# A decoder kernel: nine of each layer's weight low parts are subtracted on GpSimd instead of VectorE

## The chip, the cores and the metric

The kernel runs on one core of a Trainium2 chip. The metric is the device time of one execution in microseconds, where less is better. Three runs of the kernel before gave 1090.48, 1091.21 and 1092.42 us, so their median is 1091.21 us. The engines are named as in the profile: PE is TensorE, DVE is VectorE, ACT is ScalarE, POOL is GpSimd, SP is SyncE.

## The reference

The reference is a decoder trunk of two layers over 256 tokens of width 1024, all in float32. Cut to what matters here:

```python
for l in range(DEPTH):                       # DEPTH = 2
    h = rmsnorm(x, norm_mix[l])
    zin = h @ w_in[l]                        # 1024 x 6840, split among four mixers and four gates
    o_a = mla_branch(cq, ckv, kpe, ...)      # attention with a low-rank latent
    o_b = spatial_gating_branch(sg_uv, ...)  # gated MLP over chunks
    o_c = gla_branch(gq, gk, gv, ...)        # gated linear attention
    o_d = deltanet_branch(dq, dk, dv, ...)   # short convolution, triangular solve, recurrence
    proj = einsum('bsnw,nwd->bsnd', branches, w_branch)
    x = x + sum(sigmoid(gates) * proj) @ w_out
    x = x + cross_attention(rmsnorm(x), rmsnorm(mem), wq, wk, wv, wo)
    x = x + (relu(rmsnorm(x) @ w_up) ** 2) @ w_down
return rmsnorm(x, norm_final)
```

## The kernel before, in words

**The weights as a stream.** All weights of a layer lie in device memory in the order in which they are used, as 168 sections of 128 x 1024 float32 numbers (`N_HALF`). `half()` hands out the next section. One transfer on SP's queue (line 184) brings two sections into a raw tile `wr`, of which there are three.

**The split.** Products are made in a reduced float32 format, and to keep the precision each operand is split into a high part and a low part. For a weight section ACT copies `wr` into `wh` (line 195), which rounds it, and DVE subtracts `wh` from `wr` into `wl` (line 198). There are four `wh` and four `wl` buffers. A product is then three matmuls in `mm3`: line 202 (`wh` by the operand's high part), line 203 (`wh` by its low part) and line 204 (`wl` by its high part). Where tokens are the output rows (`gemm_tok`), `wh` and `wl` stand on the other side, and line 203 is the one that uses `wl`. A section feeds 24 matmuls of 256 columns, or 12 of 512 columns in `gemm_tok`.

**What the sections are.** Within each layer, counted from 0: 0 to 9 are the input projection for the DeltaNet inputs, a mixed group, the linear attention's q and k and the latent. 10 to 17 are output gates, the query latent and the gated MLP's u (`zin_rest`), 18 to 21 are values in token order (`gemm_tok`), 22 and 23 are the attention's up-projections (used late, in `mla`), 24 to 55 are the gates, four sections to each of eight column blocks. After that come cross attention's keys, the branch merge, the output projection, cross attention and the MLP.

**Order of the work.** Python writes the program in order, and a planner lays it out: it walks the program with a model of its own of each engine's time, takes what is ready by priority, and fixes for every engine (and SP's queue) one order, which is not changed when the kernel runs. The two halves of a split stand under `high_priority(offset=WP)` with WP = 200, so they are taken some 200 places ahead of their turn; work under `urgent` uses 400. While PE goes through sections 10 to 55, DVE, ACT and POOL also carry the four mixers (`soft_gates`, `conv`, the rotary table, the generators `dn()` and `others()`), whose small matmuls are laid between those of the gates.

**Lines the prediction speaks of.** 543 and 545: the DeltaNet convolution on DVE. 414 to 420: the angles of the rotary table, the last of them on DVE (419) ahead of a Sin on ACT (420), which needs a table load. 487 and 746: projections read from PSUM and scaled. 1081: the low part of the normalized activations. 519: a polynomial. 324: the low part of an operand with a gain. 342 and 347: sums of squares on POOL. 1116, 1117 and 1121: merging of gated branches. 1016 and 1017: parts of a GELU on POOL. 528: a minimum on POOL.

Of the kernel before, what the change touches and what calls it, by code (L numbers as in the profile page):

```python
# [9 lines left out]
F32 = mybir.dt.float32  # L10
# [3 lines left out]
ALU = mybir.AluOpType  # L14
# [16 lines left out]
N_HALF = 168  # L31
# [9 lines left out]


PAD = 48

# [22 lines left out]
def decoder(ctx: ExitStack, tc: tile.TileContext, ws, xn_d, xt_d, mem_d, pos_d, fin_d, par_d, cst_d, msk_d, out_d):  # L69
    nc = tc.nc  # L70
    V, S, G, PE = nc.vector, nc.scalar, nc.gpsimd, nc.tensor
# [10 lines left out]
    def nm(s):  # L82
        uid[0] += 1
        return f"{s}_{uid[0]}"
# [48 lines left out]

    ap.tile([P, PAD], F32, tag="pad", name="pad")

# [42 lines left out]
    def half(parts=1):  # L178
        if Stream.i % 2 == 0:
            if Stream.i < 4:  # L180
                Stream.raw = raw0[Stream.i // 2]
            else:
                Stream.raw = wp.tile([P, 2048], F32, tag="wr", name=nm("wr"), bufs=3)
                nc.sync.dma_start(Stream.raw, ws[Stream.i // 2])
        o = 1024 * (Stream.i % 2)
        Stream.i += 1
        r = Stream.raw[:, o : o + 1024]
        wh, wl = (wp.tile([P, 1024 + SLACK // 4], F32R, tag=n, name=nm(n), bufs=4) for n in ("wh", "wl"))
        b, c = (n // 4 for n in Stream.place[Stream.i % len(Stream.place)])
        wh, wl = wh[:, b : b + 1024], wl[:, c : c + 1024]  # L190
        n = 1024 // parts
        for c in range(0, 1024, n):
            p = slice(c, c + n)
            with tc.high_priority(offset=WP):
                i = S.activation(wh[:, p], r[:, p], AF.Copy)  # L195
                if Stream.i <= 4:
                    tc.keep_in_program_order(i)
                V.tensor_tensor(wl[:, p], r[:, p], wh[:, p].bitcast(F32), op=ALU.subtract)  # L198
        return wh, wl

    def mm3(out, ah, al, bh, bl, start, stop):
# [4 lines left out]
    def lead4(xh, xl, evac, pieces):  # L206

        bk = [pg.tile([P, 2, T], F32, tag="g", name=nm("g")) for _ in range(2)] + [bank() for _ in range(2)]
        for j in range(4):
            w = half(2 if j == 0 else 1)  # L210
            pieces(j)
            for m in range(4):
                for i in range(2):
                    k = 2 * j + i
                    c = slice(256 * m + 128 * i, 256 * m + 128 * i + 128)
                    mm3(bk[m][:, 0], w[0][:, c], w[1][:, c], xh(k), xl(k), k == 0, k == 7)
        for p in range(2):
            evac(p, [(slice(m, m + 1), bk[2 * p + m][:, 0:1]) for m in range(2)])

    def gemm(xh, xl, nk, npair, evac, lead=False, tail=False, first=0):  # L220

        for p in range(first, npair):
            apart = (lead and p == 0) or (tail and p == npair - 1)
            if apart:
                bk = [pg.tile([P, 2, T], F32, tag="g", name=nm("g")) for _ in range(2)]
                parts = [(slice(m, m + 1), bk[m][:, 0:1]) for m in range(2)]
                out = [bk[m][:, 0] for m in range(2)]
            else:  # L230
                ps = pg.tile([P, 2, T], F32, tag="g", name=nm("g"))
                parts = [(slice(0, 2), ps)]
                out = [ps[:, m] for m in range(2)]
            if lead and p == 0:
                w = [half() for _ in range(2)]
                order = [(m, k) for kp in range(0, 8, 2) for m in range(2) for k in (kp, kp + 1)]
            else:
                w = [None, None]
                order = [(m, k) for m in range(2) for k in range(nk)]
            for m, k in order:  # L240
                if k % 8 == 0 and not (lead and p == 0):
                    w[m] = half()
                c = slice(128 * (k % 8), 128 * (k % 8) + 128)
                mm3(out[m], w[m][0][:, c], w[m][1][:, c], xh(k), xl(k), k == 0, k == nk - 1)
            evac(p, parts)
# [1228 lines left out]
```

## Time and profile before

| what | value |
|---|---|
| runs shown | 1091.21 us median (1090.48 to 1092.42) |
| profiled execution, its own time | 1090.66 us |
| its span, first to last instruction | 1088.3 us |
| granted TensorE clock | 0.997 |
| PE busy | 1064.5 us, 98% |
| DVE busy | 812.7 us, 75% |
| ACT busy | 583.8 us, 54% |
| POOL busy | 197.6 us, 18% |
| line 198 on DVE, 337 instructions | 415.3 us |

The span stands for the kernel's instructions; 2.36 us of the execution's own time lie around it. Busy shares are means over stages that differ a great deal: the DVE is near 100% in some and near 50% in others. PE's busy time counts a matmul until its modelled end, so a PE that is busy need not be a PE at its best rate. Times in the views are microseconds from the span's start, unless marked ns.

### The profile page before, as it was taken

The page shows a single profiled execution, that of the slowest core. Times are in us where ns is not written, and L with a number is a line of the kernel's source. Part 1 is how long each engine was busy: PE and PEld are TensorE (multiplying, and loading weights), DVE is VectorE, ACT ScalarE, POOL GpSimd, SP SyncE. Part 2 cuts the span into 40 slices and gives each one's busy share as a digit, 9 for nine tenths or more (in the row PEclk, how much of TensorE's full clock was granted, in tenths as well). Part 3 has the DMA queues.
Part 4 walks back from the last instruction along what each step waited for, and adds up shares of the span by engine and source line. Part 5 has one row for each costly group of instructions (what it writes and reads, how often), then busy time and mean ns, then how long its engine had stood idle before and what let it go on. Part 6 is the DMA issues. An engine that isn't in the chain of part 4 may idle for free.

```text
span 1088.3 us, 20696 instructions
## 1 busy us (share of the span) xinstructions
PE 1064.5 (98%) x8494; PEld 1020.9 (94%) x8494; DVE 812.7 (75%) x1419; ACT 583.8 (54%) x875; POOL 197.6 (18%) x170
## 2 busy tenths in 40 slices
PE   9989999999999999999999999999999999999996
PEld 8979998899998999999999899989999899999885
DVE  7999857789866876655689997686797778665454
ACT  6565554554645666644455746544555555555342
POOL 6334005108300200000102321410451011010000
PEclk9999999999999999999999999999999999999998
DMA  9442523354544455555555343334455345554551
GB/s 364 170 173 107 207 105 122 112 194 156 194 155 155 160 195 195 194 194 194 195 188 202 140 167 141 117 144 152 171 193 194 132 142 192 194 206 165 194 191 39
DMA packets 28319, 185.13 MB, mean 170 GB/s; under 512 B 3392, under 2 KB 3648, under 8 KB 6976
## 3 DMA queue, kind: packets, MB, share of 16 engines
q1 hardware_dynamic: 26208, 179.09, 45.4%
q10 hardware_dynamic: 2016, 4.72, 1.3%
q8 instruction: 66, 1.08, 0.4%
q14 instruction: 29, 0.24, 0.1%
HBM read 182.75 MB, written 1.05 MB: 169 GB/s over the span
## 4 chain that ended last, share of the span: by engine, by line
PE 81%; DVE 11%; ACT 3%; DMA 2%; issue 1%; POOL 1%; ACTq 0%; DVEq 0%; POOLq 0%
PE g L202 24%; PE g L204 24%; PE g L203 24%; DVE wl L198 3%; DMA mr<-memt 2%; DVE qt L865 1%; PE ps L202 1%; ACT wh L195 1%; PE ps L203 1%; PE ps L204 1%; DVE gt L1116 1%; PE ps L666 1%; PE ps L670 1%; DMA wr<-ws 1%; DVE mgl L1124 1%
## 5 line engine op out<-in xcount | busy, mean ns | idle before, releaser
L198 DVE TENSOR_TENSOR wl<-wr,wh 128x1024 fp32r<-128x1024 f32 (+1 forms) x337 | 415.3, 1235 | 182.9 <-ACT wh L195 181.2
L195 ACT ACTIVATE wh<-wr 128x1024 fp32r<-128x1024 f32 (+1 forms) x337 | 355.1, 1057 | 332.9 <-PE g L203 233.8
L204 PE MATMUL g<-hh,wl 128*128 128x256 f32 x1152 | 324.0, 282 | 3.4 <-DVE wl L198 3.4
L202 PE MATMUL g<-hh,wh 128*128 128x256 f32 x1152 | 322.5, 281 | 1.9 <-ACT gt L1101 1.5
L203 PE MATMUL g<-hl,wh 128*128 128x256 f32 x1152 | 321.6, 279 | 0.0
L204 PEld LDWEIGHTS g<-hh,wl 128*128 128x128 f32 x1152 | 216.4, 188 | 5.6 <-DVE wl L198 4.4
L202 PEld LDWEIGHTS g<-hh,wh 128*128 128x128 f32 x1152 | 216.3, 188 | 3.1 <-ACT gt L1101 1.9
L203 PEld LDWEIGHTS g<-hl,wh 128*128 128x128 f32 x1152 | 218.0, 189 | 0.4 <-issue 0.2
L342 POOL TENSOR_TENSOR sq<-sq,sq 128x512 f32<-128x512 f32 x14 | 23.3, 1661 | 341.0 <-ACT sq L334 340.8
L203 PE MATMUL g<-xl,wh 128*128 128x256 f32 x272 | 75.4, 279 | 0.3 <-DVE xl L324 0.3
L202 PE MATMUL g<-xh,wh 128*128 128x256 f32 x272 | 74.8, 279 | 0.6 <-ACT xh L315 0.6
L204 PE MATMUL g<-xh,wl 128*128 128x256 f32 x272 | 74.5, 279 | 0.0
L202 PE MATMUL g<-ah,wh 128*128 128x256 f32 x256 | 70.7, 276 | 0.0
L203 PE MATMUL g<-al,wh 128*128 128x256 f32 x256 | 70.7, 276 | 0.0
L204 PE MATMUL g<-ah,wl 128*128 128x256 f32 x256 | 70.7, 276 | 0.0
L202 PEld LDWEIGHTS g<-xh,wh 128*128 128x128 f32 x272 | 50.8, 188 | 1.3 <-ACT xh L315 1.3
L1117 POOL TENSOR_TENSOR gt<-gt,gt 128x512 f32<-128x512 f32 x16 | 35.5, 2218 | 90.8 <-DVE gt L1116 89.9
L203 PEld LDWEIGHTS g<-xl,wh 128*128 128x128 f32 x272 | 51.1, 188 | 0.5 <-DVE xl L324 0.5
L204 PEld LDWEIGHTS g<-xh,wl 128*128 128x128 f32 x272 | 50.8, 189 | 0.0
L204 PE MATMUL g<-wh,al 128*128 128x512 f32 x128 | 49.5, 389 | 0.0
L203 PE MATMUL g<-wl,ah 128*128 128x512 f32 x128 | 49.5, 389 | 0.0
L202 PE MATMUL g<-wh,ah 128*128 128x512 f32 x128 | 49.4, 390 | 0.0
(500 smaller groups left out, 2331.0 us busy)
## 6 DMA issues: line engine op xcount, KB each, us to landing
wr<-ws SPq DMA_DIRECT2D x166, 1024.0 KB, 4.8
wr<-ws ACTq DMA_DIRECT2D x4, 512.0 KB, 7.5
mr<-memt ACTq DMA_DIRECT2D x8, 256.0 KB, 4.7
par<-par SPq DMA_DIRECT2D x2, 778.0 KB, 6.8
x<-xt SPq DMA_DIRECT2D x3, 256.0 KB, 7.8
cst<-cst SPq DMA_DIRECT2D x1, 588.0 KB, 8.4
gf<-fin SPq DMA_DIRECT2D x2, 256.0 KB, 5.3
yt<-yg ACTq DMA_DIRECT2D x2, 256.0 KB, 2.5
```

The source lines that it names most:

```text
L195: i = S.activation(wh[:, p], r[:, p], AF.Copy)
L198: V.tensor_tensor(wl[:, p], r[:, p], wh[:, p].bitcast(F32), op=ALU.subtract)
L202: PE.matmul(out, ah, bh, start=start, stop=False)
L203: PE.matmul(out, ah, bl, start=False, stop=False)
L204: PE.matmul(out, al, bh, start=False, stop=stop)
L342: G.tensor_tensor(acc, acc, sq, op=ALU.add)
L666: PE.matmul(xp[:, h], M[:, h], Tm[:, h], start=True, stop=True)
L670: PE.matmul(up[:, h], X[t][:, h], U[:, h], start=True, stop=True)
L865: V.tensor_tensor(qt[:, a].rearrange("p (b h) -> p b h", h=h), e3, halves(qbd[a // 2][:, a % 2], i)[:, :, 1], op=ALU.mult)
L1116: V.scalar_tensor_tensor(gt[m][a], gt[m][a], 1.0, ps, op0=ALU.add, op1=ALU.mult)
L1117: G.tensor_tensor(gt[m][0], gt[m][0], gt[m][1], op=ALU.add)
L1124: V.scalar_tensor_tensor(dl, t, 0.5, dh.bitcast(F32), op0=ALU.mult, op1=ALU.subtract)
```

## The change

In each layer, of sections 8 to 43, each one whose running count divides by four (`Stream.i` is counted from 1, so these are sections 11, 15, 19, 23, 27, 31, 35, 39 and 43) has its low part subtracted by `G`, which is GpSimd, and no longer by `V`. That is 18 of the 336 sections of the kernel. Operands, shapes and buffers are the same, and the two lines stay under the same priority.

```diff
 PAD = 48
+
+
+SHARE = range(8, 44)
@@ half()
                 i = S.activation(wh[:, p], r[:, p], AF.Copy)
                 if Stream.i <= 4:
                     tc.keep_in_program_order(i)
-                V.tensor_tensor(wl[:, p], r[:, p], wh[:, p].bitcast(F32), op=ALU.subtract)
+                (G if (Stream.i - 1) % N_HALF in SHARE and Stream.i % 4 == 0 else V).tensor_tensor(wl[:, p], r[:, p], wh[:, p].bitcast(F32), op=ALU.subtract)
         return wh, wl
```

## The prediction

> **What bounds the kernel now.** I read the page first, for the engines and the costliest groups.
>
> ```profile
> PE 1064.5 (98%) x8494; PEld 1020.9 (94%) x8494; DVE 812.7 (75%) x1419; ACT 583.8 (54%) x875; POOL 197.6 (18%) x170
> ...
> L198 DVE TENSOR_TENSOR wl<-wr,wh 128x1024 fp32r<-128x1024 f32 (+1 forms) x337 | 415.3, 1235 | 182.9 <-ACT wh L195 181.2
> ...
> L204 PE MATMUL g<-hh,wl 128*128 128x256 f32 x1152 | 324.0, 282 | 3.4 <-DVE wl L198 3.4
> ```
>
> PE is the bound, at 98%. DVE comes next, and the subtraction of line 198 is half of its work. But what PE loses to line 198 in the gates is only 3.4 us, so a relief of DVE can win a few microseconds at most. Where they lie is told by the busy time in three stretches (columns: stretch, its length, then busy PE, PEld, DVE, ACT, POOL), and then by the waits of PE from 60 to 90 us.
>
> ```profile
> 46.00:72.00 26.00, 25.20 (x174) 22.92 (x174) 25.83 (x39) 14.52 (x21) 5.20 (x5) 1.00 0.51 181
> 60.00:90.00 30.00, 26.31 (x168) 23.07 (x169) 29.45 (x56) 19.16 (x28) 11.60 (x11) 1.00 0.49 179
> 620.00:630.00 10.00, 9.05 (x80) 8.85 (x79) 9.86 (x36) 5.33 (x9) 0.00 (x0) 1.00 0.30 107
> ```
> ```profile
> PE g L204 <- DVE wl L198: 2.5, 3, 0.9
> PE g L203 <- DVE wl L198: 0.7, 1, 0.7
> PE g L202 <- ACT wh L195: 0.4, 1, 0.4
> ```
>
> From 60 to 90 us PE is idle for 30.00 - 26.31 = 3.69 us, of which 2.5 + 0.7 = 3.2 us wait for a low part and 0.4 us for a copy. From 620 to 630 it is idle for 0.95 us. DVE has no room in these places: 25.83 of 26 us, 29.45 of 30. So the change does touch the engine that ends last there. The 4.6 us are the most it can win.
>
> Inside the first layer the order of events matters. DVE runs without a pause until it makes the last angle (line 419); ACT waits for that, loads tables, and only then makes the copy of section 25, for whose halves PE waits:
>
> ```profile
> 71.15 1.26 DVE L419 TENSOR_SCALAR a<-a 32x256 f32<-32x256 f32 x1
> 72.44 1.39 DVE L198 TENSOR_TENSOR wl<-wr,wh 128x1024 fp32r<-128x1024 f32 x1
> ```
> ```profile
> 72.49 1.28 ACT L420 ACT_TABLE_LOAD   x1 [0.92 <-DVE a L419]
> ...
> 77.19 1.06 ACT L195 ACTIVATE wh<-wr 128x1024 fp32r<-128x1024 f32 x1
> ```
>
> The low part at 72.44 is section 23, which moves. What else moves ahead of 71.15 is 11, 15 and 19. Each microsecond by which line 419 comes later or earlier is a microsecond at PE behind 77.19.
>
> **What the two engines do to each other.** The change puts a two-input POOL instruction beside a full DVE. This is what the trace shows of such a pair:
>
> ```profile
> 280.64 0.48 DVE L324 SCALAR_TENSOR_TENSOR hl<-x,hh 128x256 fp32r<-128x256 f32 x1
> 281.03 1.22 DVE L198 TENSOR_TENSOR wl<-wr,wh 128x1024 fp32r<-128x1024 f32 x1
> 282.17 1.52 DVE L324 SCALAR_TENSOR_TENSOR hl<-x,x,hh 128x256 fp32r<-128x256 f32 x1
> ```
> ```profile
> 281.05 2.35 POOL L342 TENSOR_TENSOR sq<-sq,sq 128x512 f32<-128x512 f32 x1 [7.56 <-ACT sq L334]
> ```
> ```profile
> 371.23 0.96 DVE L324 SCALAR_TENSOR_TENSOR hl<-x,x,hh 128x256 fp32r<-128x256 f32 x1
> ```
> ```profile
> 370.77 1.14 POOL L347 TENSOR_TENSOR sq<-sq,sq 128x256 f32<-128x256 f32 x1 [1.21 <-ACT sq L334]
> ```
>
> Line 324 takes 0.48 us alone and 1.52 us where POOL adds 512 columns beside it: DVE stood for 1.04 us. Beside 256 columns it takes 0.96, so it stood for 0.48. The POOL instruction in its turn took 2.35 us, of which it spent up to 1.2 behind the subtraction at 281.03, which was not slowed. So the two take turns. Not every DVE instruction is held: one that reads PSUM runs on.
>
> ```profile
> 255.54 0.68 DVE L1116 SCALAR_TENSOR_TENSOR gt<-gt,g 128x512 f32<-128x512 f32 x1
> ```
> ```profile
> 254.56 2.22 POOL L1117 TENSOR_TENSOR gt<-gt,gt 128x512 f32<-128x512 f32 x1
> 256.85 0.81 POOL L1121 TENSOR_TENSOR gt<-gt 128x256 f32<-128x256 f32 x1
> ```
>
> Line 1116 reads the bank `g` and keeps its 0.68 us under POOL's 2.22.
>
> The Trainium skill's page "SBUF — State Buffer", section "Who interferes with whom", states it as a rule: GpSimd shares a port pair with a VectorE instruction that has two inputs in SBUF, whoever starts first keeps it to its end, and the other fully blocks. The trace agrees, with the 1.04 us above. Without that rule the sum below would hold no blocked time, and the result would be the first rival's.
>
> **The price of one moved subtraction.** None of 1024 columns on POOL is in the trace. For DVE, 0.48 us at 256 and 1.04 at 512 columns make about 2.1 at 1024 (twice 1.04). The lower end is 1.8: POOL's own 0.81 us at 256 (line 1121) grows to 1.15 at 512 (2.35 less the 1.20 until 282.25, when the subtraction ended), 0.34 per 256 columns, so 1.15 + 2 x 0.34. The upper end is 2.2, by a straight line through DVE's losses (1.04 + 2 x 0.56). I take 2.1, as DVE's losses are what the sum is made of. The page "GPSIMD Engine Reference" of the Trainium skill, section "Performance versus the Vector engine", has 4497 ns for 2048 columns, so 2.25 us by estimate; with that the sum below would be about 1 us more.
>
> What DVE gets back is 1.1 us:
>
> ```profile
> 49.63 1.22 DVE L198 TENSOR_TENSOR wl<-wr,wh 128x1024 fp32r<-128x1024 f32 x1
> 50.76 0.88 DVE L543 SCALAR_TENSOR_TENSOR cv<-zc,par,cv 128x254 f32<-128x254 f32 x2
> 51.55 0.69 DVE L746 TENSOR_TENSOR og<-g,rrow 128x512 f32<-128x512 f32 x1
> ```
> ```profile
> 61.12 1.78 DVE L514 RECIPROCAL sp<-sp 128x264 f32<-128x264 f32 x1
> 62.83 1.15 DVE L198 TENSOR_TENSOR wl<-wr,wh 128x1024 fp32r<-128x1024 f32 x1
> ```
>
> Section 15 stands at 49.63 and the next starts at 50.76: 1.13 us. Section 19 is at 62.83. Of the 26 us from 46 to 72, four instructions like line 746's (0.6 each) and the reciprocal (1.7) don't hold POOL up or wait for it, 4.1 us or 16%. So a hold costs DVE 0.84 x 2.1 = 1.76 us on average.
>
> **The sum, part by part.**
>
> First layer, up to line 419:
> - Section 11: POOL would have it from the end of its copy, while DVE reads banks (32.80 below, and its like), so I let the hold cost 0.5, and 1.2 us go away at 36.77: -0.7.
>
> ```profile
> 32.80 0.68 DVE L487 TENSOR_TENSOR zc<-g,rrow 128x512 f32<-128x512 f32 x1
> ...
> 36.77 1.21 DVE L198 TENSOR_TENSOR wl<-wr,wh 128x1024 fp32r<-128x1024 f32 x1
> ```
>
> - Sections 15 and 19: 1.76 - 1.13 each, +1.3 together.
> - Section 23: its copy ends at 67.76, so its hold falls ahead of line 419, and its 1.1 us are given back only behind it: +1.76. But line 419 took 1.26 us because POOL's line 1017 stood beside it; that one is now queued behind the subtraction. Line 324 takes 0.48 for as many columns, so -0.78. Together +1.0.
>
> ```profile
> 66.70 1.06 ACT L195 ACTIVATE wh<-wr 128x1024 fp32r<-128x1024 f32 x1 [1.46 <-PE g L204]
> ```
> ```profile
> 70.13 2.13 POOL L1017 TENSOR_TENSOR ge<-ge,su 128x512 f32<-128x512 f32 x1
> ```
>
> That is +1.6 at PE behind 77.19. PE's earlier waits are swallowed by this one and count for nothing.
>
> First layer, section 27: at this point two of the four buffers are held by sections 22 and 23, and PE waits for each low part as it is made.
>
> ```profile
> 83.38 1.04 ACT L195 ACTIVATE wh<-wr 128x1024 fp32r<-128x1024 f32 x1
> ```
> ```profile
> 85.17 1.19 DVE L198 TENSOR_TENSOR wl<-wr,wh 128x1024 fp32r<-128x1024 f32 x1
> ```
>
> The copy ends at 84.42. DVE ended the low part at 86.36; POOL would, after some 0.3 us behind DVE, at 84.7 + 2.1 = 86.8: +0.4.
>
> Second layer, section 11: its copy ends at 568.98, POOL gets its turn within 0.7 us (what 512 columns take on DVE, as in line 746) and DVE stands until about 571.8.
>
> ```profile
> 567.91 1.07 ACT L195 ACTIVATE wh<-wr 128x1024 fp32r<-128x1024 f32 x1
> ```
> ```profile
> 571.58 1.22 DVE L198 TENSOR_TENSOR wl<-wr,wh 128x1024 fp32r<-128x1024 f32 x1
> ```
> ```profile
> 573.32 0.39 PE L204 MATMUL g<-xh,wl 128*128 128x256 f32 x2
> ```
>
> The subtraction at 571.58 is section 10's, done at 572.79; the second matmul of the last row (573.43) is the first that needs it. It has 0.64 us to spare and comes 1.76 late: +1.1. Its section 27, in the same place as the first layer's, gets half of that one's price, +0.2, as PE waits there for section 26 already (the 0.95 us). The others (15, 19 and 23 here, 31 to 43 of both layers) I cost at nothing: the page's 3.4 us are all found above, so PE waits for none of them, and what covers them is the queue of gates that PE has ahead of them. Were that gone, each would cost 2.1 - 1.1 = 1.0.
>
> The sum is 1.6 + 0.4 + 1.1 + 0.2 = +3.3 us. With 1.8 or 2.2 for the hold it is 1.9 or 3.8 (0.25 less or 0.08 more on each of sections 15, 19 and 23 and on the second layer's 11, 0.3 or 0.1 on each 27). The profiled execution took 1090.66 us (its span 1088.3 and 2.4 around it), which is 0.55 below the median shown, so I set it on the median: 1091.2 + 3.3 = **1094.5 us**. No transfer is added or moved; SP's queue keeps its order, though a raw tile is released by POOL for these sections.
>
> **The rivals.**
> - *Relief reaches PE.* The new fixed orders put the holds where DVE reads PSUM or rests, and PE gets back what it waits for: 3.2 + 0.4 + 0.95 us, less 0.4 and 0.2 for the two sections 27 and 0.6 for waits that follow PE's own buffers, about -3.3: 1087.9. For it: DVE is full where PE waits, POOL is at 18%. Against: the 1.04 us. Chance 0.27. It decides from a hold under 1.1 us.
> - *A wash.* Half of each hold falls beside PSUM reads: about 1.05 lost against 1.13 won per section, and section 27's lateness remains: 1091 to 1092.5. Chance 0.25.
> - *Worse.* DVE's loss adds up through the second layer (15, 19 and 23 each +1.0 until section 24, whose low part in the first layer is one of those that PE waits 0.9 us for): +3.0 more, 1097.5. Chance 0.10.
> - *Not done as said.* The code moves 18 of 336 and can't do less, but the planner lays every queue anew, which can shift waits of a microsecond or so anywhere; that is in the ranges.
>
> **How the numbers follow.** The forecast has 0.38. With its own range of 1092.5 to 1096.5 it is likeliest. The range over all cases, 1088.0 to 1097.4, leaves a tenth out on each side. A difference under 0.2% (2.2 us) can't be told from none: slower takes the forecast but for its low end (0.35) and the worse case (0.10), 0.45; faster is the first rival but for its small gains and a part of the wash, 0.29; the rest, 0.26, is the same.
>
> **What would show it.** Right: POOL rows on line 198, 2.1 us and more, 3 with waiting; DVE rows of lines 543, 545 or 1081 beside them longer by 1 to 2 us; line 419 later than 71.15; PE idle from 60 to 90 over 3.69 us. Wrong: the moved rows under 1.6 us, DVE's rows unstretched, PE's wait at section 19 gone and none in its place.

## The result, and the profile after

The changed kernel takes 1108.86 us (median of three runs, 1108.17 to 1109.21) against 1091.21: 17.65 us more, a ratio of 1.0158 with a 95% interval of 1.0144 to 1.0173. The forecast was 1094.5 us in a range of 1088.0 to 1097.4. The sign was the one given the highest chance; the size was five times the sum. The profiled execution took 1108.86 us (span 1106.7). Three lines were added at the head of the file, so line 198 of before is 201 here, 202 to 204 are 205 to 207, and so on.

The page of the changed kernel, engines and costliest groups:

```profile
PE 1071.0 (97%) x8494; PEld 1027.8 (93%) x8494; DVE 821.8 (74%) x1401; ACT 582.4 (53%) x875; POOL 238.7 (22%) x188
...
L201 DVE TENSOR_TENSOR wl<-wr,wh 128x1024 fp32r<-128x1024 f32 (+1 forms) x319 | 392.6, 1233 | 186.1 <-ACT wh L198 184.5
L207 PE MATMUL g<-hh,wl 128*128 128x256 f32 x1152 | 324.8, 282 | 9.1 <-DVE wl L201 8.6
...
L207 PE MATMUL g<-xh,wl 128*128 128x256 f32 x272 | 76.0, 281 | 5.6 <-DVE wl L201 5.6
...
L201 POOL TENSOR_TENSOR wl<-wr,wh 128x1024 fp32r<-128x1024 f32 x18 | 47.5, 2638 | 83.4 <-ACT wh L198 83.4
```

DVE's subtractions cost 415.3 - 392.6 = 22.7 us less, and yet DVE is busy for 821.8 - 812.7 = 9.1 us *more*. So its other instructions became 31.8 us longer, 1.77 for each of the 18 moved. PE's wait for low parts made by DVE grew from 3.4 to 8.6 us in the gates, and from nothing to 5.6 us in the input projection. For POOL's own low parts PE waits 0.6 us in all, and ACT waits 1.4 us for weights to land (1.6 before). So neither POOL's slower subtraction itself nor a late transfer is where the time goes.

Where PE lost it, by stretches (columns: stretch, length, busy PE, PEld, DVE, ACT, POOL, granted clock, DMA share, GB/s). First the changed kernel, then the kernel before for the two stretches that the prediction did not look at:

```profile
46.00:72.00 26.00, 21.76 (x149) 20.12 (x147) 25.78 (x38) 11.48 (x16) 6.46 (x6) 0.93 0.43 162
60.00:90.00 30.00, 25.25 (x154) 22.54 (x155) 28.87 (x54) 19.34 (x29) 10.78 (x10) 0.94 0.48 175
100.00:130.00 30.00, 27.43 (x229) 26.88 (x227) 28.07 (x93) 14.96 (x23) 10.61 (x8) 0.94 0.31 115
...
614.00:650.00 36.00, 30.69 (x216) 28.25 (x214) 33.30 (x86) 19.11 (x41) 16.33 (x14) 0.91 0.39 141
```
```profile
100.00:130.00 30.00, 30.00 (x261) 29.78 (x258) 29.14 (x98) 16.06 (x22) 3.50 (x4) 1.00 0.40 145
614.00:650.00 36.00, 35.05 (x304) 34.16 (x305) 34.45 (x116) 19.02 (x34) 8.56 (x9) 1.00 0.39 143
```

From 60 to 90 us PE is idle for 4.75 us (3.69 before), from 46 to 72 for 4.24 (0.80), from 100 to 130 for 2.57 (none), from 614 to 650 for 5.31 (0.95). A second thing stands in these rows: the granted clock was 1.00 in all of them before and is 0.91 to 0.94 now.

The hold itself, as the timeline shows it on DVE and on POOL (start, length, instruction):

```profile
44.59 2.51 DVE L417 SCALAR_TENSOR_TENSOR a<-a,a 64x256 f32<-64x256 f32 x1
...
49.96 1.66 DVE L546 SCALAR_TENSOR_TENSOR cv<-zc,par,cv 128x254 f32<-128x254 f32 x4
...
54.87 0.52 DVE L417 SCALAR_TENSOR_TENSOR a<-a,a 64x256 f32<-64x256 f32 x1
...
56.42 3.84 DVE L546 SCALAR_TENSOR_TENSOR cv<-zc,par,cv 128x253 f32<-128x253 f32 x4
60.18 1.21 DVE L201 TENSOR_TENSOR wl<-wr,wh 128x1024 fp32r<-128x1024 f32 x1
```
```profile
44.08 2.75 POOL L201 TENSOR_TENSOR wl<-wr,wh 128x1024 fp32r<-128x1024 f32 x1 [9.33 <-ACT wh L198]
...
56.76 2.42 POOL L201 TENSOR_TENSOR wl<-wr,wh 128x1024 fp32r<-128x1024 f32 x1 [0.60 <-ACT wh L198]
```

Line 417 takes 0.52 us alone and 2.51 beside POOL's subtraction; four of line 546 take 1.66 and then 3.84. Each hold is 2.0 to 2.2 us. Behind the second one stands the subtraction at 60.18 for section 17, and this is what PE does meanwhile, and what its clock does next:

```profile
61.44 0.39 PE L207 MATMUL g<-xh,wl 128*128 128x256 f32 x1 [2.68 <-DVE wl L201]
```
```profile
59.41:62.82 3.41, 1.38 (x12) 1.38 (x13) 3.41 (x6) 2.21 (x3) 0.00 (x0) 1.00 0.16 24
62.82:66.23 3.41, 3.41 (x16) 3.22 (x15) 3.35 (x5) 1.01 (x1) 0.00 (x0) 0.50 0.93 372
...
643.09:646.50 3.41, 1.61 (x14) 1.41 (x14) 3.29 (x8) 1.06 (x1) 1.78 (x2) 1.00 0.00 0
646.50:649.91 3.41, 3.41 (x18) 3.41 (x18) 2.81 (x11) 0.00 (x0) 0.00 (x0) 0.50 0.74 264
```

In the 3.41 us behind the stall PE has a granted clock of 0.50 and starts 16 matmuls, about half of the 32 that it starts in a full window at full clock in experiment 4. This happens four times, from 62.82, 114.02, 622.61 and 646.50, each time for 3.41 us. The kernel before has no such stretch until its last one at 1082.2.

### The profile page after: what moved, and what is told of

The parts are those of the page before. It is cut to its first block, busy times and chain, and to the rows that moved or that the text cites. A ratio compares the mean times of both kernels' runs of the same rounds, so it can differ in the third digit from the quotient of the medians.

```text
span 1106.7 us, 20697 instructions
## 1 busy us (share of the span) xinstructions
PE 1071.0 (97%) x8494; PEld 1027.8 (93%) x8494; DVE 821.8 (74%) x1401; ACT 582.4 (53%) x875; POOL 238.7 (22%) x188
## 4 chain that ended last, share of the span: by engine, by line
PE 78%; DVE 14%; ACT 3%; issue 2%; DMA 1%; POOL 1%; ACTq 0%; POOLq 0%
PE g L207 23%; PE g L206 23%; PE g L205 23%; DVE wl L201 4%; ACT wh L198 1%; DVE gt L1119 1%; DVE mgl L1127 1%; DVE cv L546 1%; PE ps L205 1%; PE ps L207 1%; PE ps L206 1%; DMA mr<-memt 1%; DMA wr<-ws 1%; DVE qt L868 1%; DVE w L649 1%
## 5 line engine op out<-in xcount | busy, mean ns | idle before, releaser
L201 DVE TENSOR_TENSOR wl<-wr,wh 128x1024 fp32r<-128x1024 f32 (+1 forms) x319 | 392.6, 1233 | 186.1 <-ACT wh L198 184.5
L207 PEld LDWEIGHTS g<-hh,wl 128*128 128x128 f32 x1152 | 218.9, 190 | 11.3 <-DVE wl L201 9.8
L201 POOL TENSOR_TENSOR wl<-wr,wh 128x1024 fp32r<-128x1024 f32 x18 | 47.5, 2638 | 83.4 <-ACT wh L198 83.4
```

The costliest lines, as they stand in the source:

```text
L201: (G if (Stream.i - 1) % N_HALF in SHARE and Stream.i % 4 == 0 else V).tensor_tensor(wl[:, p], r[:, p], wh[:, p].bitcast(F32), op=ALU.subt ...
L207: PE.matmul(out, al, bh, start=False, stop=stop)
```

## Experiments

**Theories.** One: the hold; POOL's subtraction keeps DVE from its operands for about 2 us, and PE has less reserve than the forecast gave it. Two: the planner's new order hands low parts over later. Three: whichever it is, a stall of 2 us costs up to 1.7 us again through the clock (half of 3.41 us).

To tell one from two, the order was taken out of the planner's hands. A kernel's orders were read off as lists of instruction names, and written into another as dependencies that cost nothing when it runs:

```diff
+def _written_order(tc):
+    for names in ORDER:                  # TensorE, VectorE, ScalarE, GpSimd
+        for a, b in zip(names, names[1:]):
+            tc.add_manual_dep(b, a, NoSync)
```

**1. The hold against the order.** The move in the old order differs from the changed kernel only by such lists. For the fill, POOL writes zeros in place of the subtraction, in the one and in the other order:

```diff
+    if <one of the 18 sections>:
+        G.memset(wl[:, p].bitcast(F32), 0.0)
+    else:
         V.tensor_tensor(wl[:, p], r[:, p], wh[:, p].bitcast(F32), op=ALU.subtract)
```

> The 18 subtractions are on GpSimd, but VectorE, ScalarE, TensorE and GpSimd keep the order that the kernel before has on each of them; the planner places only the 18. Theory 1 (the hold: each moved subtraction keeps VectorE from its operands for about 2 us, and TensorE has no reserve there): the loss of 17.65 us stays, 1105 to 1110 us. Theory 2 (the planner's new order hands the low parts over later): the order is the old one, so what is left is the forecast's own sum, 1091 to 1095 us. Theory 3 (an amplifier for either: TensorE's granted clock is 0.5 for 3.41 us behind a stall of 2 us or more, about 1.7 us each): as many half-clock stretches as there are such stalls, four under theory 1, none under theory 2.

> As the run above in its order, but for the 18 sections GpSimd fills the low part with zeros in place of the subtraction: it writes the same 128x1024 tile and reads nothing. The low parts of these 18 sections are left out of the result. VectorE is relieved of 18 x 1.1 us, and a fill needs no operand from SBUF. Theory 1: no hold, so only the relief is left, 1087.5 to 1091 us, and VectorE's rows of 0.5 us beside a fill stay at 0.5 us. Theory 2: the old order, also 1087.5 to 1091 us. If it is slower than 1093 us, the cost lies in GpSimd's start and hand-over and both theories fall.

> The fill in place of the 18 subtractions, with every engine, GpSimd too, in the order of the changed kernel; the low parts of the 18 sections are left out of the result. Theory 1: the hold is gone, and with it the loss: 1088 to 1092 us. Theory 2: the order is what costs, so most of it stays: 1103 to 1108 us. Theory 3: with theory 1 no half-clock stretch before the last stage, with theory 2 two to four.

A fourth corner was run later: everything subtracted on DVE, in the new order.

> All 336 sections are subtracted on VectorE again, but TensorE, ScalarE and GpSimd and the other work of VectorE stand in the order of the changed kernel; the planner places only the 18 subtractions on VectorE. With the fill, the new order was 2.6 us faster than the old one (1085.55 against 1088.14), about what its two half-clock stretches fewer are worth. The hold as the whole cause: nothing is held, nothing relieved, so the time of the kernel before within a few microseconds, 1089 to 1094 us. If the new order is bad in itself and only the relief hid that under the fill: 1095 us or more.

Medians in us, with the ratio to the kernel before of the same chip (1091.7, and 1091.38 for the last) and its interval:

| 18 low parts | old order | new order |
|---|---|---|
| subtracted on VectorE | the kernel before | 1094.31, 1.0026 (1.0017 to 1.0036) |
| filled by GpSimd | 1088.14, 0.9971 (0.9958 to 0.9983) | 1085.55, 0.9947 (0.9928 to 0.9966) |
| subtracted on GpSimd | 1100.9, 1.0088 (1.0065 to 1.0111) | 1108.86, the changed kernel |

The column of the new order tells the two apart. With every instruction in the changed kernel's order, reading nothing on POOL takes 23.3 us off and leaves a kernel 6 us *faster* than before. A fill is also shorter than a subtraction and needs no copy from ACT, but PE waited only 0.6 us for POOL's low parts, so that is not where the 23.3 us come from. Theory two falls as a cause by itself: without a hold the new order costs 2.9 us. But it isn't neutral. The move in the old order, 1100.9, lay between what the two theories had given; the subtraction in place of the fill costs 1100.9 - 1088.14 = 12.8 us in the old order and 23.3 in the new. In the fill, DVE's row beside POOL stays short (first DVE, then POOL, then PE's group of the gates, of the fill in the new order; line numbers are 3 higher than in the changed kernel):

```profile
43.78 0.42 DVE L420 SCALAR_TENSOR_TENSOR a<-a,a 64x256 f32<-64x256 f32 x1
```
```profile
42.87 0.96 POOL L202 MEMSET wl<- 128x1024 f32 x1 [10.09 <-PE g L210]
```
```profile
L210 PE MATMUL g<-hh,wl 128*128 128x256 f32 x1152 | 323.3, 281 | 4.3 <-DVE wl L204 4.3
```

The Trainium skill's page "SBUF — State Buffer", section "Who interferes with whom", says that a VectorE instruction with two SBUF inputs contends with a GpSimd instruction that reads SBUF and not with one that only writes it. This trace agrees: 0.42 us beside the fill, 2.51 beside the subtraction. It is not true of every instruction of DVE. A copy with one input, 0.22 us long in the kernel before, is held to the end of a fill (DVE, then POOL, of the same kernel):

```profile
80.93 1.01 DVE L646 COPY w<-cst 128x128 f32<-128x128 f32 x1
```
```profile
80.90 0.96 POOL L202 MEMSET wl<- 128x1024 f32 x1 [2.30 <-PE g L210]
```

Such cases are few: in the fill in the old order DVE's instructions beside the 18 fills are 2.8 us longer than in the kernel before, and beside the 18 subtractions in that order 28.8.

Theory three is seen in the count of half-clock stretches ahead of the last stage: none in the move in the old order, four in the changed kernel, two and none in the fills (old and new order). Four times 1.7 us would be 6.8 of the 8.0 us between the two moves. Set against the fill in the same order, the changed kernel's matmuls fall back by 1.6, 1.3, 1.6 and 1.5 us within the four stretches, 6.0 together, and don't catch up behind them. That is not always so: in the kernel with ten sections of experiment 3 a stretch from 78.52 makes PE 1.5 us later, and the next wait, near 82.5, takes that in.

**2. The hold without the relief.** DVE keeps all its subtractions, and POOL subtracts the same 18 sections once more for nobody:

```diff
     V.tensor_tensor(wl[:, p], r[:, p], wh[:, p].bitcast(F32), op=ALU.subtract)
+    if <one of the 18 sections>:
+        G.tensor_tensor(twice, r[:, p], wh[:, p].bitcast(F32), op=ALU.subtract)
```

> VectorE keeps all of its subtractions, in the old order on every engine, and GpSimd also subtracts the same 18 sections into a tile that nobody reads. Nothing is handed over by GpSimd, and VectorE is relieved of nothing. Theory 1: the hold alone, on a VectorE that is 18 x 1.1 us fuller than in the changed kernel: 1106 to 1116 us. Theory 2: nothing of the order has changed, 1090 to 1093 us.

Measured: 1122.28 us, 1.0287 (1.0265 to 1.0308): 30.6 us for work that hands nothing to anybody, more than the 1106 to 1116 us that theory one gave. The clock has a part in it, as its profile has seven windows at 0.50 ahead of the last stage. The raw tiles are read for longer too, but ACT waits 1.8 us for weights to land (1.6 before), so that is not the cause. Every engine of before keeps its order here, so each DVE instruction can be set beside its own self in the kernel before. Beside the 18 additional subtractions DVE's instructions became 31.1 us longer: thirteen times by 1.8 to 2.2 us, otherwise by less, and not at all in the last, beside which DVE had a single instruction. One pair, DVE then POOL:

```profile
45.99 3.38 DVE L201 TENSOR_TENSOR wl<-wr,wh 128x1024 fp32r<-128x1024 f32 x1
```
```profile
45.91 2.38 POOL L203 TENSOR_TENSOR twice<-wr,wh 128x1024 f32<-128x1024 f32 x1 [9.66 <-ACT wh L198]
```

A subtraction of 1.22 us, asked for 0.08 us after POOL's, takes 3.38: it is held until POOL's ends.

**3. Which sections.** The move in the old order, for the eight sections that the forecast costed at nothing, and for the ten others (`SHARE = range(28, 44)` and `range(8, 28)`):

> Only sections 31, 35, 39 and 43 of each layer are subtracted on GpSimd, the eight that the forecast costed at nothing; every engine keeps the old order. If the gates queued ahead of TensorE cover them, as the forecast says: 1090 to 1093 us. If each hold counts by itself where it falls: what the full move in the old order lost at sections 32 to 34 of the first layer (1.9 us) and at 33 of the second (2.0 us), so 1095 to 1097 us. If those losses were only a backlog that the earlier eight holds had left on VectorE: 1091 to 1093 us, as with cover.

> The complement: only sections 11, 15, 19, 23 and 27 of each layer on GpSimd, in the old order. If each hold counts where it falls: 1100.9 less the 3.9 us of the late sections, 1096 to 1098 us, and late and early losses add up to that of the full move (9.2 us). If VectorE's backlog carries the loss into the late sections: 1099 to 1101 us. By the forecast's own sum: 1094 to 1096 us.

Measured: 1095.07 us, 1.0033 (1.0021 to 1.0046), and 1099.65, 1.0082 (1.0064 to 1.0100), by medians 3.7 and 8.3 us over the kernel before. So the eight are not covered. Nor are they a backlog of the ten, though 1099.65 lies where the expectation had put a backlog. PE's instructions stand in the same order in all of these, so each matmul's lateness (how much later it starts than in the kernel before) can be read. For the last ones it is 3.5 us for the eight, 8.3 for the ten and 11.95 for all 18, nearly the sum; the medians, 3.7, 8.3 and 9.2, add up less well. Where the eight lose it was a surprise. PE's waits for low parts are nearly the same as before (4.5 us, 4.1 before), and for those made by POOL it doesn't wait at all. In the second layer all of the loss, 2.0 us, comes at one point, which is no wait for a weight (DVE, POOL and PE of the kernel with the eight; then the first of these in the kernel before):

```profile
650.44 2.35 DVE L648 TENSOR_TENSOR w<-w 128x40 f32<-128x40 f32 x1
652.71 0.15 DVE L289 SCALAR_TENSOR_TENSOR rmy<-rmt,rmy 128x4 f32<-128x4 f32 x1
```
```profile
650.07 2.66 POOL L201 TENSOR_TENSOR wl<-wr,wh 128x1024 fp32r<-128x1024 f32 x1 [5.70 <-ACT wh L198]
```
```profile
653.01 0.41 PE L308 MATMUL ps<-cst,rmy 128*128 128x128 f32 x2 [1.82 <-DVE rmy L289]
```
```profile
647.95 0.20 DVE L645 TENSOR_TENSOR w<-w 128x40 f32<-128x40 f32 x1
```

A small product of the triangular solve, 0.20 us, is held for 2.15. Behind it on DVE waits the last step of a root (line 289), and for that the transposition of line 308, which stands in PE's order ahead of the next gates. In the first layer it is the same kind of thing twice: a step of another root (0.15 us, held to 2.37) makes PE 0.75 us later at 113.65, and line 941 (0.41, held to 2.63) another 0.76 at 120.55, where PE waits for `ck`. Neither is a wait for a weight.

**4. The clock.** 15 stalls of growing length were put into a stage where PE never waits in the kernel before; its matmuls there are also kept in program order:

```diff
         def ev_up(p, parts):
+            if l == 0 and p:
+                V.tensor_copy(x, parts[0][1][:, 0, 0:1])
+                <GpSimd scales 96 * p columns by x into c>
+                <a small matmul of c, in program order on TensorE>
```

> The kernel before with 15 stalls made for TensorE in a stage where it otherwise never waits (the first layer's up projection, two halves of a pair apart): behind pair p VectorE copies one element of the bank, GpSimd scales 96 x p columns by it, and a small product of the result stands between the pairs in TensorE's fixed order. By 0.98 us for 512 columns on GpSimd and some 0.8 us of hand-over (an estimate from the rows of GpSimd and VectorE) the stalls grow from about 1.0 to 3.6 us, 34 us together. Theory 3, as the changed kernel's four half-clock stretches and its 2.15-us gap without one suggest: TensorE's clock is judged in free-running windows of 3.413 us, and one in which it stood for some 2 us or more is followed by 3.41 us at 0.5; stalls under 1.9 us never do it, those of 3 us and more mostly do, those between only where they fall within one window: 5 to 9 stretches, 1125 us and 1.7 us for each, 1133 to 1140 us. The rule that a whole window must be idle (the Trainium skill's page 'TensorE: Matmul & The Clock Gate', on when the clock drops): no stretch, or one behind the longest stalls, 1122 to 1128 us.

Measured: 1170.41 us beside 1090.31, one run each, so the time was missed by 30 us. 14 stalls of 0.89 to 4.90 us came out, 40.6 together, longer than estimated, as GpSimd took 1.56 to 1.67 us for 512 columns and not 0.98. Twelve half-clock stretches stand ahead of the last stage and not 5 to 9, five of them two windows long. Two are at none of the made stalls: one near 175 us, and one of two windows from 376.36, behind waits of 3.40 and 2.62 us for a norm ahead of the stage, which the kernel before doesn't have. The ten made stalls of 1.90 us and more have one each, the four shorter ones none. The windows around three stalls (columns as above):

```profile
413.91:417.32 3.41, 2.35 (x21) 2.34 (x22) 2.15 (x3) 1.55 (x3) 1.01 (x1) 1.00 0.28 46
417.32:420.73 3.41, 3.41 (x32) 3.33 (x30) 1.23 (x1) 1.06 (x1) 0.00 (x0) 1.00 0.63 262
420.73:424.15 3.42, 1.52 (x14) 1.39 (x13) 2.65 (x4) 2.22 (x3) 1.49 (x1) 1.00 0.05 10
424.15:427.56 3.41, 3.41 (x19) 3.41 (x18) 0.00 (x0) 0.41 (x1) 0.00 (x0) 0.50 0.78 298
427.56:430.97 3.41, 2.70 (x23) 2.50 (x22) 1.83 (x3) 1.44 (x2) 0.35 (x1) 1.00 0.00 0
430.97:434.39 3.42, 1.53 (x13) 1.51 (x14) 2.10 (x3) 1.43 (x3) 1.75 (x2) 1.00 0.20 43
434.39:437.80 3.41, 3.41 (x18) 3.41 (x17) 0.00 (x0) 0.59 (x1) 0.00 (x0) 0.50 0.64 269
```

A window with 1.06 us of idle PE is followed by 32 matmuls at full clock, one with 1.90 by 19 at half. The stall from 430.26 to 432.86 lay across two windows, with 0.71 and 1.89 us of idle PE in them, and only the second was followed by half clock. All stretches of a run lie on one grid of 3.413 us. Over the profiles of eleven kernels (before, changed, those of experiments 1 to 4 and the first of experiment 5), between 12 and 1040 us and by the modelled ends of the matmuls, all 20 windows at full clock with 1.86 us or more of idle PE were followed by half clock, 4 of the 11 between 1.50 and 1.86, and of those with 1.0 to 1.5 only one. That one is in the changed kernel: a stall of 2.72 us up to 620.54 lay across two windows with 1.38 and 1.35 us of idle PE, and the stretch from 622.61 follows. Idle time alone is not the whole rule. In the kernel that has both moves of experiment 5, laid out anew by the planner, the clock fell at 76.31 behind a window with 0.12 us of idle PE, in which 16 products of two columns make up 1.9 us of the busy time. The Trainium skill's page "TensorE: Matmul & The Clock Gate", section "What's actually happening", has the free-running window of 3413 ns, which the rows agree with, and has the clock drop after a window of idleness; here a little over half a window of idle time was enough, and the measurement decides.

**5. A version that is faster than both?** The fill shows what relief without a hold is worth, but leaves work out. Five kernels try to take away the holds that the kernel before has already: POOL's one-input instructions to ACT (there are twelve of them, not ten), its two-input ones to DVE, both, and the last two again with the rest in the old order.

```diff
-            G.tensor_scalar(R.la, y[:, :, 0:128], 0.0, None, op0=ALU.min)
+            S.activation(R.la, y[:, :, 0:128], AF.Relu, scale=-1.0)
...
-                G.tensor_tensor(w, w, z, op=ALU.mult)
+                V.tensor_tensor(w, w, z, op=ALU.mult)
```

> The kernel before without the move, and with four one-input GpSimd instructions of each layer's gates and gelu (min with 0, plus 2, times 1/15, times 0.044715 plus 1) made on ScalarE instead: ten instructions of 0.8 to 2.3 us fewer on GpSimd, 15 us of its busy time. If every GpSimd instruction that reads SBUF holds VectorE for about its own time where VectorE is full, the dense stretches get shorter: 1086 to 1089.5 us. If only the two-input ones hold it, or ScalarE's copies come later for it: 1091 to 1095 us.

> The kernel before with the opposite move: 22 two-input GpSimd instructions of the two layers (the products and sums of the gelu branch, the causal mask of the decay, the rotated key, the masked queries: 28 us of GpSimd) are made on VectorE instead, where by its rows of 0.68 us for 512 and 0.41 us for 256 columns they cost 13 us. If an instruction on GpSimd takes more from VectorE than VectorE needs for it itself (2.1 us of hold against 1.13 us for a subtraction of 1024 columns, 1.04 against 0.68 for 512), this is faster than before by 0.3 us for each that falls where VectorE is full: 1086 to 1090 us. If these 22 mostly stand beside reads of PSUM, where the hold costs nothing: 1091 to 1096 us.

> The 22 two-input instructions on VectorE and the ten one-input ones on ScalarE: GpSimd reads next to nothing from SBUF in the input projection and the first gates. If the holds of these 32 are what VectorE loses there: 1085 to 1089 us. If they cost nothing where they stand: 1091 to 1097 us, by VectorE's 13 us and ScalarE's ten instructions.

> As the run that put 22 two-input GpSimd instructions on VectorE, but TensorE, ScalarE, GpSimd and the rest of VectorE keep the old order, and the planner places only the 22. In the run without that, TensorE's waits for a low part in the gates fell from 3.4 to 0.9 us and VectorE's busy time fell in spite of 22 more instructions; the 4 us of loss stood at the end of the DeltaNet branch (stalls of 1.29 and 2.10 us near 171 and 173, 1.83 near 706) with half-clock stretches behind them. If a hold takes more from VectorE than the instruction itself and only the new order spoiled it: 1086.5 to 1089.5 us, with no half-clock stretch behind 171. If VectorE's longer queue delays the branch by itself: 1092 to 1095 us.

> The 22 two-input instructions on VectorE and the twelve one-input ones on ScalarE, the rest in the old order. If the holds of these 34 are what counts: 1085.5 to 1089 us, at or below the run with the 22 alone. If ScalarE's copies of the weights come later for the twelve: above it.

Measured, as ratios to the kernel before: 1.0010 (1.0000 to 1.0019), 1.0036 (1.0023 to 1.0048), 1.0039 (1.0026 to 1.0051), and in the old order 1.0013 (1.0004 to 1.0022) and 1.0017 (1.0008 to 1.0026). None is faster. With the 22 on DVE in the old order PE was 0.8 us earlier by 104 us, and 1.3 us later at one low part near 622. So the idea that a two-input instruction on POOL costs DVE more than making it itself is not borne out for these 22. They cost it just as much: in the old order DVE is busy for 812.6 us with the 22 on it, 13.9 us of its own rows, and for 812.7 without. Whether each stands where a hold costs little was not traced.

## Why the prediction was right or wrong

**The hold: right.** The forecast had 2.1 us for one hold, from 0.48 and 1.04 us at 256 and 512 columns; the traces show 2.0 to 2.2. It had 1.76 per section after a share that meets reads of PSUM; the changed kernel's profile gives 31.8 / 18 = 1.77, and the additional subtractions 31.1 / 18 = 1.73. POOL's own row is 2.42 us when it waits for nothing, over the 2.25 that was estimated from the Trainium skill's page "GPSIMD Engine Reference", section "Performance versus the Vector engine".

**The relief: about right.** "Relief reaches PE" was priced at 1087.9 us, 3.3 us under before; the fill in the old order, where nearly nothing is held, took 1088.14, by medians 3.6 us under. That they are so near is in part luck: in the profiled execution of the fill PE's last matmuls are only 2.0 us earlier than before.

**The sum over sections: the step that failed first.** The kernel with the move in the old order lets it be answered place by place, by PE's lateness at each section (to the end it is 12.0 us; the profiled executions themselves, 1102.0 and 1090.66 us, are 11.3 apart, the medians 9.2):

| what moves | forecast, us | PE's lateness gained, us |
|---|---|---|
| first layer, 11 | -0.7 | +0.2 |
| 15 and 19 | +1.3 | +1.6 |
| 23 | +1.0 | +1.0 |
| 27 | +0.4 | +0.6 |
| 31 to 43 | 0 | +1.9 |
| second layer, 11 | +1.1 | +1.3 |
| 15, 19 and 23 | 0 | +1.1 |
| 27 | +0.2 | +1.0 |
| 31 to 43 | 0 | +1.8 |
| other stages | 0 | +1.5 |
| sum | +3.3 | +12.0 |

Where the forecast had found a wait or a spare time of PE, the terms were within 0.3 us, save the first layer's section 11, whose relief of 0.7 never reached PE, and the second layer's 27. What was wrong is the sentence "The others ... I cost at nothing: the page's 3.4 us are all found above, so PE waits for none of them, and what covers them is the queue of gates". It took a wait of nothing for a reserve without end, and it looked at low parts alone. These eleven sections cost 4.8 us in the table, against nothing forecast. In the second layer PE comes to wait 1.1 us, at 617.77, for a low part that it had never waited for. In the kernel with only the eight late sections the queue of gates did cover the low parts; but DVE was held also on small products of the mixers, and for those PE waits in its fixed order: at 653.01 for a root, behind a held product of 0.2 us. The forecast put the kernel at 1094.5 us; with the order held it came to 1100.9.

A smaller slip stands in the forecast's own bounds: with "0.3 or 0.1 on each 27" the low sum is 1.7 and not 1.9, which comes out if the second layer's 27 counts half.

**"The planner lays every queue anew, which can shift waits of a microsecond or so anywhere": the second step that failed.** With the hold, the new order cost 8.0 us more than the old. It stood section 17's low part behind four held instructions of line 546 (60.18), and PE's longest waits grew from 1.8 us in the old order to 2.7 (at 61.44 for that low part, at 620.54 for a small operand `g`). The new order by itself was worth 2.9 us to the bad with all on DVE and 2.6 to the good with the fill.

**The clock: missing from the forecast.** The prediction says nothing of it, as the clock before was 1.00 in every row it quoted. Four stretches at 0.50 are 6.0 us by PE's lateness (6.8 if each counts 1.7), about a third of the 17.65. What is left of the 8.0 us, some 2, was not traced further.

**The signs.** POOL's rows of 2.1 us and more, up to 3 with waiting, came (mean 2.64); lines 546 and 417 were longer by 2 us; PE's idle time from 60 to 90 rose to 4.75. "Line 419 later than 71.15" did not come in the changed kernel, where that instruction (422) stands at 70.79, as the new order takes it earlier. In the old order it comes at 76.15 (DVE, then ACT):

```profile
69.70 3.42 DVE L201 TENSOR_TENSOR wl<-wr,wh 128x1024 fp32r<-128x1024 f32 x1
...
76.15 0.37 DVE L422 TENSOR_SCALAR a<-a 32x256 f32<-32x256 f32 x1
```
```profile
75.16 1.28 ACT L423 ACT_TABLE_LOAD   x1
...
79.97 1.05 ACT L198 ACTIVATE wh<-wr 128x1024 fp32r<-128x1024 f32 x1
```

"Each microsecond by which line 419 comes later or earlier is a microsecond at PE behind 77.19" did not hold even there. The line ends 4.1 us later (72.41 before, 76.52 now), but the copy of section 25 starts only 2.8 us later than 77.19, and so does PE: ACT now loads its table while it waits for the angle, and in the kernel before it did so behind the angle (72.49).

"PE's earlier waits are swallowed by this one and count for nothing" failed in the new order: line 422 comes 0.36 us *earlier* than before there, and yet PE is about 5.5 us late at section 25, nearly all of it from section 17, behind which it is 5.4 us late already.

**The rivals.** The one called *worse* (1097.5, a chance of 0.10) saw that the second layer's 15, 19 and 23 are not free, but priced them at +1.0 each (measured +1.1 for the three) and saw nothing behind them. No rival held the result; the range ended 11 us short.

## What to carry to other kernels

Before work goes from a full engine to an idle one, ask what the two share: here each two-input subtraction on GpSimd took 1.75 us from VectorE and gave 1.1 to 1.3 back, and the same move without reads was 6 us faster than the kernel before. Cost a delay also where the profile shows no wait: find how much later a result may come, and what else stands in order behind the instruction that is held. And reckon with up to 1.7 us more for a stall of TensorE of about 2 us, since the clock was often 0.50 for the 3.4 us behind one.

## What the runs showed of the hardware that was not expected

- TensorE's granted clock fell to 0.50 for one window of 3.413 us behind each window with 1.86 us or more of idle TensorE (20 of 20 in eleven kernels), not only behind an empty one. Between 1.50 and 1.86 us both were seen (4 of 11 fell). A row of two-column products, busy in the profile, did not keep the clock up either. As the grid of the windows lies anew in each execution, a stall of 2.15 us from 78.50 to 80.65 in the changed kernel fell across two windows, with 1.11 and 0.77 us of idle time in them, and no half clock followed.
- A fill of 128x1024 by GpSimd (0.96 us) held none of VectorE's two-input instructions shown, and now and then one with one input (a copy of 0.22 us took 1.01), while the subtraction of the same tile (2.42 us) held a two-input instruction to its end.
- In the output projection of the cross-attention, matmuls came every 118 ns in the changed kernel, the move in the old order, the additional subtractions and the kernel with all on VectorE in the new order, and every 113 in the kernel before, both fills and the kernels with eight and ten sections, with the same instructions: 0.8 us in each layer. Most of the table's "other stages" is that, and so is about half of the 2.9 us of the new order with all on VectorE. As it comes without the move too, it is not the hold's; its cause is open.
